# A hybrid decoder layer on one core: x handed over a second time with k on the partitions, norm factors as columns, row scale later

## The chip, the cores and the metric

The kernel runs on one core of one Trainium2 chip. It uses five engines: TensorE (PE) multiplies 128x128 weights with up to 512 columns and writes to PSUM, VectorE (DVE) and ScalarE (ACT) do element-wise work, GpSimd (POOL) makes masks and issues some transfers, and SyncE (SP) issues most transfers. In this kernel the operand that PE loads first ("LDWEIGHTS") is a block of activations, and the model's weights stream past it. The metric is the device time in microseconds (us) of one execution.

## The reference

One decoder layer, sequence 256, width 2048, float32. Cut to what matters here:

```python
h = rmsnorm(x, g_mix)                      # x * rsqrt(mean(x*x) + eps) * g_mix
proj = h @ w_in                            # 2048 x (3 * 2048 + 3 * 2048)
q, k, v = ...                              # 16 heads of 128
gates = sigmoid(proj[..., 3 * MIX_WIDTH:]) # three gates of 2048 channels
o_a = stick_breaking_attention(q[:, :4], k[:, :4], v[:, :4])
qn, kn = rmsnorm(q[:, 4:], q_gain), rmsnorm(k[:, 4:], k_gain)
o_b = moba_attention(...)                  # 6 heads, with a relative-position bias
o_c = dilated_attention(...)               # 6 heads, with a relative-position bias
merged = sum of gates[i] * (o_i @ w_branch[i])
x = x + merged @ w_out
gu = rmsnorm(x, g_ffn) @ w_gu
x = x + (silu(gu[..., :D_FF]) * gu[..., D_FF:]) @ w_down
```

## The kernel before, in words

All matrix products keep float32 accuracy by splitting each operand into a high part (a rounding cast to the type fp32r, on ACT) and a low part (the rest, subtracted on DVE), and adding three products: high x high, high x low, low x high (`product`, lines 159 to 162). A weight tile is two k-tiles of 128 rows by 512 columns (512 KB), loaded on SP into one of four `w_raw` buffers, split into five `w_hi` and five `w_lo` buffers (`split`, line 106), and used for two row tiles of 128 tokens. So a k-tile costs PE six matmuls.

`h` holds the activations with k on the partitions, as high and low parts: 16 k-tiles of 128 rows by 256 tokens. The norm is applied in two pieces. The channel factor g_mix multiplies x on the way into `h`; the token factor `rstd` (one number for each row) is applied later, to the results in PSUM, since a row scale commutes with the product. `rstd` comes from sums of squares of x as rows (`squares`, on ACT), a reduction and `rsqrt_mean` (a logarithm, an exponential and two refinement steps, DVE and ACT in turn).

The input projection goes in units: V of the heads 0 to 3, a gate chunk, Q and K of heads 0 to 3, and so on (`units`). V and gate units are plain (`project`); two units side by side use one level of a seven-product scheme on k-tiles 0 to 7 (`project_pair`, begun early by `begin_pair`), whose sums of activations are made by `sums_of_h` from the k-tiles times g_mix. Four PSUM banks (`ps`, `qs`, two of each) take turns; V unit 0 has `ps`, gate unit 0 `qs`, and the first Q/K pair `ps` again, so that pair cannot begin before V has been read out and scaled by `keep_v`.

x arrives as rows. Each of its eight pieces (128 tokens by 512 channels) is turned by four PE transposes through a PSUM tile `tr`, multiplied by g1 (g_mix as columns) on DVE, or on ACT for the last channels, and split. For the first four k-tiles the order of PE, DVE and ACT is written out by hand (lines 472 to 504: `high`, `low`, `first_columns`, `low_part`, `high_high`, `low_high`, `high_low`), weights coming one k-tile at a time. g_mix arrives as 16 rows of 128 and is turned by one PE transpose (line 446); the FFN factor and the gains of q and k arrive as 40 rows on POOL's queue and are turned later (line 591). `idle` puts filler matmuls of zeros on PE, five and then three.

Other work is cut into small steps (generators in `stages` and `slow_stages`) that are advanced once per k-tile or weight tile; a scheduler then orders each engine's instructions by its own estimate, apart from those marked `keep_in_program_order`. Transfers by `fetch` keep their place on SP.

Of the kernel before, what the change touches and what calls it, by code (L numbers as in the profile page):

```python
# [17 lines left out]
P = 128  # L18
D = 2048
S = 256  # L20
# [14 lines left out]
NDIST = 3 * P - 1  # L35

# [18 lines left out]
def hybrid_block(ctx: ExitStack, tc: tile.TileContext, x, g_mix, w_in, q_gain, k_gain, w_branch, w_out,  # L55
                 g_ffn, w_gu, w_down, rel_bias, onehot, extra, out):
# [12 lines left out]
    consts.tile([P, 72], F32, name="fill")  # L69
    gmix = consts.tile([KT, P], F32, name="gmix")  # L70
    nc.scalar.dma_start(gmix, g_mix[0].rearrange("(k p) -> k p", p=P))
# [43 lines left out]
    def weights(w, row0, k0, nk, col0, there=()):  # L115

        for i, c in enumerate(range(k0, nk, 2)):
            raw = there[i] if i < len(there) else raw_weights(w, row0, c, col0)[0]
# [21 lines left out]
    def project(acts, k0, w, row0, nk, col0, ps=None, done=0, there=(), last=1):  # L140
# [4 lines left out]
        for k, w_hi, w_lo in weights(w, row0, done, nk, col0, there):  # L145
# [234 lines left out]

    NPAR = KT + 2 * H_SOFT
    par = consts.tile([NPAR, P], F32, name="par")
# [22 lines left out]
    def to_h(acts, src, c, t, g, by_scalar=False):  # L405

        pt = transpose4(src)
        tmp = half_kb().rearrange("p (k q) -> p k q", k=4)
        if by_scalar:
            for i in range(4):  # L410
                nc.scalar.activation(tmp[:, i], pt[:, i], AF.Copy, scale=g[:, 4 * c + i:4 * c + i + 1])
        else:
            nc.vector.tensor_mul(tmp, pt, g[:, 4 * c:4 * c + 4, None].to_broadcast([P, 4, P]))
        acts.put(c, t, tmp)
        return tmp

    def squares(xc, dst, c, pin=False):
        for t in range(NT):
            sq = nc.scalar.activation(half_kb(), xc[t], AF.Square, accum_out=dst[:, t, c:c + 1])
            if pin:  # L420
                tc.keep_in_program_order(sq)
# [3 lines left out]
    g1 = consts.tile([P, KT], F32, name="g1")  # L425
    g2 = consts.tile([P, KT], F32, name="g2")
# [4 lines left out]
    xc = [half_kb() for _ in range(NT)]  # L431
    xs = [xc]
    raws = [wpool.tile([P, 2, NB], F32, name="w_raw", bufs=4) for _ in range(2)]

    def first_weights(k):
        fetch(raws[k // 2][:, k % 2, :], w_in[k * P:(k + 1) * P, V0:V0 + NB])
# [8 lines left out]
    pg = tr.tile([P, 4 * P], F32, name="tr")  # L445
    nc.tensor.transpose(pg[:, :KT], gmix, ident[:KT, :KT])
    nc.vector.tensor_copy(g1, pg[:, :KT])
    xs.append(load_x(1, fetch))
    there = []
    for k in (4, 6):  # L450
        raw, issue = raw_weights(w_in, 0, k, V0)
        tc.keep_in_program_order(issue)
        there.append(raw)
    xs += [load_x(c, fetch) for c in (2, 3)]


    columns = {c: [o_raw[:, 4 * i + 2 * t:4 * i + 2 * t + 2, :].rearrange("p h (a q) -> p (h a) q", a=2)
                   for t in range(NT)] for i, c in enumerate(WC)}

    def next_columns(c, t, pt):  # L460
        tmp = columns[c][t]
        nc.vector.tensor_mul(tmp, pt, g1[:, 4 * c:4 * c + 4, None].to_broadcast([P, 4, P]))
        h.put(c, t, tmp)

    held = []

    def first_columns(t, n, w, goes_on=None):

        if not goes_on:
            held.append(tr.tile([P, 4, P], F32, name="tr"))  # L470
            for i in range(w):
                nc.tensor.transpose(held[-1][:, i, :], xc[t][:, (n + i) * P:(n + i + 1) * P], ident)
            if goes_on is not None:
                return
        pt = held[-1]
        k = slice(n, n + w)
        c = columns[0][t][:, k]
        nc.vector.tensor_mul(c, pt[:, 0:w], g1[:, k, None].to_broadcast([P, w, P]))
        nc.scalar.copy(h.hi[:, k, t * P:(t + 1) * P], c)

    def low_part(t):
        q = slice(t * P, (t + 1) * P)
        nc.vector.tensor_sub(h.lo[:, 0:4, q], columns[0][t], h.hi[:, 0:4, q].bitcast(F32))

    ps0 = banks()
    his, los = ([wpool.tile([P, 2, NB], F32R, name=f"w_{n}") for _ in range(2)] for n in ("hi", "lo"))
    W_HI, W_LO = ([t[k // 2][:, k % 2] for k in range(4)] for t in (his, los))
    RAW = [raws[k // 2][:, k % 2] for k in range(4)]
    how = dict(skip_group_check=True, stop=False)

    def high(k):
        nc.scalar.copy(W_HI[k], RAW[k])

    def low(k):
        nc.vector.tensor_sub(W_LO[k], RAW[k], W_HI[k].bitcast(F32))

    def high_high(t, k):
        nc.tensor.matmul(ps0[t], h.plain(t, k)[0], W_HI[k], start=k == 0, **how)

    def high_low(t, k):  # L500
        nc.tensor.matmul(ps0[t], h.plain(t, k)[0], W_LO[k], start=False, **how)

    def low_high(t, k):
        nc.tensor.matmul(ps0[t], h.plain(t, k)[1], W_HI[k], start=False, **how)

    with tc.manual_schedule(engines={mybir.EngineType.PE, mybir.EngineType.DVE, mybir.EngineType.Activation}):
        high(0)
        first_columns(0, 0, 2)
        first_columns(0, 2, 2)
        idle(3)  # L510
        high_high(0, 0)
        first_columns(1, 0, 4, False)
        low(0)
        high(1)
        high_high(0, 1)
        low_part(0)
        high_low(0, 0)
        low_high(0, 0)
        first_columns(1, 0, 4, True)
        low(1)  # L520
        low_high(0, 1)
        high_low(0, 1)
        turned = [transpose4(xs[1][0])]
        high_high(1, 0)
        high_high(1, 1)
        high_low(1, 0)
        high(2)
        low_part(1)
        high_low(1, 1)
        low_high(1, 0)  # L530
        low_high(1, 1)
        low(2)
        high_high(0, 2)
        low_high(0, 2)
        turned.append(transpose4(xs[1][1]))
        high_high(1, 2)
        low_high(1, 2)
        high(3)
        low(3)
        next_columns(1, 0, turned[0])  # L540
        high_low(0, 2)
        high_low(1, 2)
        high_high(0, 3)
        low_high(0, 3)
# [552 lines left out]
```

## Time and profile before

| | |
|---|---|
| median of 3 runs | 1434.06 us (1432.44 to 1434.29) |
| the profiled execution | 1433.64 us, span 1431.9 us |
| PE busy | 1421.7 us, 99% of the span |
| VectorE, ScalarE busy | 1196.0 us (84%), 882.0 us (62%) |
| PE's clock as granted | 1.00 |
| data moved | 310.09 MB, 217 GB/s on average |
| first product of V unit 0 | 7.23 us after the span's start |
| first product of the first Q/K pair | 56.49 us |

A row of the timeline has the start, the length, the engine, the line of the kernel, the operation, the tile written and the tiles read, the shape, a count of like instructions in a row, and in brackets the idle time before it and what ended that. PE's matmuls overlap, so their lengths do not add up: what one costs is the distance from its start to the next one's start. "PEld" is the loading of the operand that stays in place, "SPq" or "ACTq" the issue of a transfer by that engine. A row of the windows has, for each engine, the busy time in that stretch, then the clock, the share of the transfer engines and GB/s.

### The profile page before, as it was taken

To read this page: it belongs to the slowest core of one execution; us is meant where nothing else is said; L and a number is where in the kernel's file an instruction comes from. 1 tells how busy PE (TensorE), PEld (TensorE's weight loads), DVE (VectorE), ACT (ScalarE), POOL (GpSimd) and SP (SyncE) were. 2 spreads that over 40 slices of the span, in tenths; PEclk is the share of its full clock that TensorE was granted. 3 is DMA by queue.
4 is the path that set the end of the run, shared out by engine and by line. 5 is a ranking of instruction groups with operands and counts; after the bars stand their busy time and mean duration, and the time that the engine had idled before them with its cause. 6 is when DMAs were issued, how large, how long until landed. Compare 5 with 4: busy or idle time off the path is not lost. (4 is left out here: it accounts for less than half of the span.)

```text
span 1431.9 us, 17773 instructions
## 1 busy us (share of the span) xinstructions
PE 1421.7 (99%) x6404; PEld 1172.1 (82%) x6404; DVE 1196.0 (84%) x1262; ACT 882.0 (62%) x1140; POOL 72.6 (5%) x133
## 2 busy tenths in 40 slices
PE   9999999999999999999999999999999999999998
PEld 7888888888788888888888888888888888788887
DVE  7888787857999886776689999999999998886775
ACT  7667876766766665444456666666666666554453
POOL 1000000000000002100100000000000010100000
PEclk9999999999999999999999999999999999999999
DMA  8763647465666758866786657666665666767552
GB/s 270 264 218 119 220 127 247 122 221 173 215 203 238 257 194 291 278 224 211 223 299 224 224 206 251 216 225 229 219 217 191 231 212 223 256 230 240 190 169 97
DMA packets 154472, 310.09 MB, mean 217 GB/s; under 512 B 10672, under 2 KB 12288, under 8 KB 154384
## 3 DMA queue, kind: packets, MB, share of 16 engines
q1 hardware_dynamic: 143200, 275.29, 57.1%
q0 software_dynamic: 10000, 32.62, 6.5%
q10 hardware_dynamic: 1184, 1.06, 0.2%
q8 instruction: 50, 0.82, 0.2%
q14 instruction: 38, 0.31, 0.1%
HBM read 292.65 MB, written 16.27 MB: 216 GB/s over the span
## 5 line engine op out<-in xcount | busy, mean ns | idle before, releaser
L106 DVE TENSOR_TENSOR w_lo<-w_raw,w_hi 128x1024 fp32r<-128x1024 f32 x334 | 406.0, 1221 | 91.1 <-ACT w_hi L106 87.5
L106 ACT CAST w_hi<-w_raw 128x1024 fp32r<-128x1024 f32 x334 | 349.0, 1052 | 166.1 <-PE qs L162 67.4
L106 ACT CAST w_hi<-g_raw 128x1024 fp32r<-128x1024 f32 x184 | 192.6, 1053 | 120.4 <-PE ps L162 39.4
L106 DVE TENSOR_TENSOR w_lo<-g_raw,w_hi 128x1024 fp32r<-128x1024 f32 x184 | 219.6, 1220 | 36.1 <-ACT w_hi L106 35.2
L106 ACT CAST w_hi<-u 128x1024 fp32r<-128x1024 f32 x138 | 144.9, 1053 | 136.1 <-DVE u L303 65.1
L106 DVE TENSOR_TENSOR w_lo<-u,w_hi 128x1024 fp32r<-128x1024 f32 x138 | 166.5, 1221 | 37.0 <-ACT w_hi L106 35.6
L161 PE MATMUL ps<-w_lo,h_hi 128*128 128x512 f32 x360 | 140.9, 392 | 0.0
L162 PE MATMUL ps<-w_hi,h_lo 128*128 128x512 f32 x360 | 140.5, 390 | 0.0
L160 PE MATMUL ps<-w_hi,h_hi 128*128 128x512 f32 x360 | 137.5, 393 | 0.0
L161 PE MATMUL qs<-w_lo,h_hi 128*128 128x512 f32 x332 | 130.0, 392 | 0.8 <-DVE w_lo L106 0.8
L162 PE MATMUL qs<-w_hi,h_lo 128*128 128x512 f32 x332 | 129.6, 390 | 0.0
L160 PE MATMUL qs<-w_hi,h_hi 128*128 128x512 f32 x332 | 126.7, 391 | 0.0
L303 DVE TENSOR_TENSOR u<-u,g_raw 128x1024 f32<-128x1024 f32 x80 | 94.4, 1218 | 0.0
L162 PEld LDWEIGHTS ps<-w_hi,h_lo 128*128 128x128 f32 x360 | 67.6, 188 | 14.0
L161 PEld LDWEIGHTS ps<-w_lo,h_hi 128*128 128x128 f32 x360 | 67.6, 188 | 13.7
L160 PEld LDWEIGHTS ps<-w_hi,h_hi 128*128 128x128 f32 x360 | 67.5, 188 | 13.7
L161 PEld LDWEIGHTS qs<-w_lo,h_hi 128*128 128x128 f32 x332 | 62.4, 188 | 13.9 <-DVE w_lo L106 1.2
L162 PEld LDWEIGHTS qs<-w_hi,h_lo 128*128 128x128 f32 x332 | 62.4, 188 | 13.4 <-issue 0.6
L160 PEld LDWEIGHTS qs<-w_hi,h_hi 128*128 128x128 f32 x332 | 62.3, 188 | 12.7
L314 DVE TENSOR_TENSOR u<-g_raw 128x1024 f32<-128x1024 f32 x40 | 48.8, 1219 | 21.0 <-DMA g_raw<-in_w_in 16.2
L160 PE MATMUL v<-w_hi,h_hi 128*128 128x512 f32 x120 | 47.5, 396 | 0.2 <-ACT w_hi L106 0.2
L161 PE MATMUL v<-w_lo,h_hi 128*128 128x512 f32 x120 | 47.1, 393 | 0.0
(397 smaller groups left out, 2935.2 us busy)
## 6 DMA issues: line engine op xcount, KB each, us to landing
w_raw<-in_w_in SPq DMA_DIRECT2D x118, 512.0 KB, 4.6
g_raw<-in_w_gu SPq DMA_DIRECT2D x88, 512.0 KB, 5.1
w_raw<-in_w_gu SPq DMA_DIRECT2D x88, 512.0 KB, 6.4
g_raw<-in_w_in SPq DMA_DIRECT2D x72, 512.0 KB, 5.8
w_raw<-in_w_down SPq DMA_DIRECT2D x64, 512.0 KB, 4.6
w_raw<-in_w_branch SPq DMA_DIRECT2D x32, 512.0 KB, 5.1
w_raw<-in_w_out SPq DMA_DIRECT2D x32, 512.0 KB, 4.7
g_raw<-in_w_down SPq DMA_DIRECT2D x24, 512.0 KB, 5.3
```

Of the source, the lines that this page charges most:

```text
L106: for op in nc.scalar.copy(hi, src), nc.vector.tensor_sub(lo, src, hi.bitcast(F32)):
L160: nc.tensor.matmul(ps, ah, wh, start=start, stop=False, **how)
L161: nc.tensor.matmul(ps, ah, wl, start=False, stop=False, **how)
L162: nc.tensor.matmul(ps, al, wh, start=False, stop=stop, **how)
L303: tc.keep_in_program_order(nc.vector.tensor_add(d, d, a))
L314: nc.vector.tensor_add(d, a, b)
```

## The change

The program is handed two more arrays instead of four small ones: `xT`, x once more with the channel within a k-tile on the partitions (128 x 16 x 256), and `gains`, the norm factors and gains as 56 columns on 128 partitions.

- The 32 transposes of x and their copies are gone from the start. `xT` is loaded into `x_raw` (the memory of `o_raw`, which the attention fills later). ACT makes the high part as x times g1 rounded (`x_high`), DVE the low part as x times g1 minus the high part in one instruction (`x_low`), 256 columns each.
- g1, g2 and the gains are slices of the one tile `par`, loaded on ACT's queue. Their transposes on PE, their copies on DVE and three loads on POOL's queue are gone.
- The first eight k-tiles instead of four come one by one, x and weights in turn on SP. The hand-written order is the same for each: x high, weight high, x low, weight low, then six products. There are seven filler matmuls ahead of it instead of eight in two groups.
- The remaining eight k-tiles of x come in two transfers of four and are split one per step of V unit 0 (`rest_of_x`).
- x as rows is still needed for the sums of squares. It is loaded within gate unit 0 (`first_norm`), between its weights on SP, followed by the squares and `rsqrt_mean`; the scaling of V 0 (`scaled` in `keep_v`) comes after that, as a step of gate unit 0.
- `sums_of_h` multiplies `x_raw` by g1 in place, and splits a chunk for both row tiles in one instruction where it took two.

In the order as built, the relative-position bias table's three loads stand first on POOL's queue, its matmul stands between products of k-tile 3 and the addition after it ahead of the low part of weight tile 6; before, the table came in gate unit 0. From the end of the first Q/K pair on, every engine has the same instructions in the same order in both kernels.

```diff
+    consts.tile([P, 344], F32, name="fill")
+    par = consts.tile([P, NPAR], F32, name="par")
+    nc.scalar.dma_start(par, gains)
+    g1, g2, q_gain, k_gain = (par[:, a:b] for a, b in zip(PAR_AT, PAR_AT[1:]))
...
-    tc.keep_in_program_order(nc.gpsimd.dma_start(par[0:KT, :], g_ffn[0].rearrange("(k p) -> k p", p=P)))
-    tc.keep_in_program_order(nc.gpsimd.dma_start(par[KT:KT + H_SOFT, :], q_gain[0]))
-    tc.keep_in_program_order(nc.gpsimd.dma_start(par[KT + H_SOFT:NPAR, :], k_gain[0]))
...
+    FIRST = 8
+    raws, his, los = ([wpool.tile([P, 2, NB], dt, name=f"w_{n}", bufs=bufs) for _ in range(FIRST // 2)]
+                      for n, dt, bufs in (("raw", F32, 4), ("hi", F32R, 5), ("lo", F32R, 5)))
+    x_raw = o_raw
+    def fetch_x(k, n):
+        fetch(x_raw[:, k:k + n, :], xT[:, k:k + n, :])
-    fetch(xc[0], x[0:P, 0:NB])
-    first_weights(0)
-    fetch(xc[1], x[P:S, 0:NB])
-    for k in range(1, 4):
-        first_weights(k)
-    idle(5)
+    for k in range(FIRST):
+        fetch_x(k, 1)
+        fetch(RAW[k], w_in[k * P:(k + 1) * P, V0:V0 + NB])
+    fetch_x(FIRST, 4)
+    idle(7)
+    def x_high(k):
+        nc.scalar.activation(h.hi[:, k, :], x_raw[:, k, :], AF.Copy, scale=g1[:, k:k + 1])
+    def x_low(k):
+        nc.vector.scalar_tensor_tensor(h.lo[:, k, :], x_raw[:, k, :], g1[:, k:k + 1], h.hi[:, k, :].bitcast(F32),
+                                       op0=ALU.mult, op1=ALU.subtract)
...
+        for k in range(FIRST):
+            x_high(k)
+            nc.scalar.copy(W_HI[k], RAW[k])
+            x_low(k)
+            nc.vector.tensor_sub(W_LO[k], RAW[k], W_HI[k].bitcast(F32))
+            for lo, w in ((0, W_HI), (1, W_HI), (0, W_LO)):
+                for t in range(NT):
+                    nc.tensor.matmul(ps0[t], h.plain(t, k)[lo], w[k], start=k + lo == 0 and w is W_HI, **how)
     def rest_of_x():
+        fetch_x(FIRST + 4, 4)
+        for k in range(FIRST, KT):
+            x_high(k)
+            x_low(k)
+            yield
+    def first_norm():
+        rows = []
+        for c in range(4):
+            rows.append(load_x(c, fetch))
+            yield
+            if c:
+                squares(rows[c - 1], ss1, c - 1)
+            yield
+        squares(rows[3], ss1, 3)
+        yield
         sst = small.tile([P, NT], F32, name="sst", bufs=1)
         nc.vector.tensor_reduce(sst, ss1, op=ALU.add, axis=AX.X)
         rsqrt_mean(rstd, sst, D, NT)
+        yield
     def sums_of_h():
+        for _ in range(2):
+            yield
         for c in WC:
-            sums(*columns[c], True)
-            yield
-            for t in range(NT):
-                split(*[x[:, :, t * P:(t + 1) * P] for x in hs.s[c]], columns[c][t])
-                yield
+            chunk = x_raw[:, 4 * c:4 * c + 4, :]
+            tc.keep_in_program_order(nc.vector.tensor_mul(chunk, chunk, g1[:, 4 * c:4 * c + 4, None].to_broadcast([P, 4, S])))
+            yield
+            sums(*(chunk[:, :, t * P:(t + 1) * P] for t in range(NT)), True)
+            yield
+            split(*hs.s[c], chunk)
+            yield
...
     def keep_v(g, ps):
+        if g:
+            finish_stages(slow_stages)
         heads["v", g] = v = pa.tile([P, NT, NB], F32, name="v", bufs=1)
+        def scaled():
+            for t in range(NT):
+                nc.scalar.activation(v[:, t, :], ps[t], AF.Copy, scale=rstd[:, t:t + 1])
+            yield
         if g:
+            finish_stages([scaled()])
             slow_stages.append(attention(g, *heads["qk", g], v))
+        else:
+            stages.extend((first_norm(), scaled()))
```

More of the change, by code (lines that the diff above doesn't have):

```diff
@@ L113, in raw_weights, with weights @@
         return raw, nc.sync.dma_start(raw, src)
-    def weights(w, row0, k0, nk, col0, there=()):
-        for i, c in enumerate(range(k0, nk, 2)):
-            raw = there[i] if i < len(there) else raw_weights(w, row0, c, col0)[0]
+    def weights(w, row0, k0, nk, col0):
+        for c in range(k0, nk, 2):
+            raw = raw_weights(w, row0, c, col0)[0]
             hi = wpool.tile([P, 2, NB], F32R, name="w_hi")
@@ L138, in finish_stages, with project @@
             advance(queue)
-    def project(acts, k0, w, row0, nk, col0, ps=None, done=0, there=(), last=1):
+    def project(acts, k0, w, row0, nk, col0, ps=None, done=0, last=1):
         ps = ps or banks()
         held = []
-        for k, w_hi, w_lo in weights(w, row0, done, nk, col0, there):
+        for k, w_hi, w_lo in weights(w, row0, done, nk, col0):
             if k:
@@ L403, in load_x, with squares @@
         return xc
[L405 to L417, printed above, removed]
+    def squares(xc, dst, c):
@@ L446, in hybrid_block @@
[L446 to L479, printed above, removed]
@@ L500, in high_low @@
[L500 to L504, printed above, removed]
-    with tc.manual_schedule(engines={mybir.EngineType.PE, mybir.EngineType.DVE, mybir.EngineType.Activation}):
[L507 to L544, printed above, removed]
-        high_high(1, 3)
-        low_high(1, 3)
-        next_columns(1, 1, turned[1])
-        high_low(0, 3)
-        high_low(1, 3)
@@ L839, in hybrid_block @@
             keep_v(what, ps)
-            if what == 0:
-                slow_stages.append(sums_of_h())
         elif kind == "qk":
```

65 lines of the change are left out of this document (17 added, 48 removed).

## The prediction

> **What bounds the kernel now.** I read the page's table of engines first, then the waits of TensorE, then the timeline of the first 60 us, which is where the diff acts.
>
> ```profile
> PE 1421.7 (99%) x6404; PEld 1172.1 (82%) x6404; DVE 1196.0 (84%) x1262; ACT 882.0 (62%) x1140; POOL 72.6 (5%) x133
> ...
> PE qs L161 <- DVE w_lo L106: 1.4, 3, 0.8
> PE ps L160 <- ACT v L773: 0.6, 1, 0.6
> ```
>
> PE is busy 99%, and from 110 us to the end (the two wait rows are the largest there) it waits under 4 us in all. So PE is the bound everywhere after the start: work taken from PE, or an earlier first product, moves the end by as much, unless a new wait gives it back. A faster VectorE or ScalarE alone is worth nothing.
>
> ```profile
> 1.52 2.50 PE L378 MATMUL tr<-sc 128*128 128x512 f32 x5 [1.52 <-DVE sc L396]
> ...
> 5.18 0.62 ACT L492 CAST w_hi<-w_raw 128x512 fp32r<-128x512 f32 x1 [2.64 <-DMA w_raw<-in_w_in]
> ...
> 5.78 1.65 PE L378 MATMUL tr<-sc 128*128 128x512 f32 x3
> ...
> 7.31 0.62 ACT L492 CAST w_hi<-w_raw 128x512 fp32r<-128x512 f32 x1 [0.71 <-DMA w_raw<-in_w_in]
> ...
> 15.49 0.48 PE L160 MATMUL ps<-w_hi,h_hi 128*128 128x512 f32 x1
> ...
> 54.68 0.39 PE L161 MATMUL qs<-w_lo,h_hi 128*128 128x512 f32 x1
> ...
> 56.49 0.39 PE L160 MATMUL ps<-w_hi,h_hi 128*128 128x512 f32 x1
> ```
>
> The row at 15.49 is the first product of k-tile 4 of the first V unit. Until then PE has done 24 products (4 k-tiles, 2 row tiles, 3 each); the rest was filler, waiting and transposes. The row at 56.49 is the first product of the first Q/K pair, after V unit 0 and gate unit 0 (192 products). From the end of that pair on, the built order of every engine is the same in both kernels, so the forecast is: when does that product start in the changed kernel?
>
> **What leaves PE, and what stays.**
>
> ```profile
> 16.27 0.40 PE L160 MATMUL ps<-w_hi,h_hi 128*128 128x512 f32 x1
> ...
> 18.11 0.39 PE L162 MATMUL ps<-w_hi,h_lo 128*128 128x512 f32 x1
> 18.34 1.03 PE L182 MATMUL tr<-ident,sc 128*128 128x128 f32 x8
> 19.13 0.48 PE L160 MATMUL ps<-w_hi,h_hi 128*128 128x512 f32 x1
> ...
> 23.58 0.60 PE L182 MATMUL tr<-ident,sc 128*128 128x128 f32 x4
> 23.93 0.48 PE L161 MATMUL ps<-w_lo,h_hi 128*128 128x512 f32 x1
> ...
> 25.27 0.25 PE L591 MATMUL tr<-ident,par 40*128 40x40 f32 x1
> ...
> 37.70 0.81 PE L605 MATMUL tr<-sc 32*12 32x383 f32 x2
> ```
>
> A product costs its spacing, not its duration: 16.27 to 18.11 is 8 steps, 0.23 us each; 54.68 to 56.49 again 8, 0.226 each. Eight transposes cost 19.13 - 18.34 = 0.79 us, four 23.93 - 23.58 = 0.35. After 15.49 the change so removes 1.14 us for twelve transposes and about 0.25 for the parameter one. The other twenty and that of the factors stood before 15.49. The bias-table matmul (0.81 us) stays; it moves from 37.70 to between two products of k-tile 3. So the changed kernel needs, from its first product to the first Q/K product, 96 x 0.23 + 96 x 0.226 + 0.8 = 44.6 us.
>
> **When the first product can start.** Its inputs: x k-tile 0 (128 KB, SP's first issue), weight tile 0 (SP's second, as before), and now the factors, one DMA of 128 rows of 224 bytes on ACT's queue, for ScalarE multiplies x by them.
>
> ```profile
> 0.81 0.38 SPq L103 DMA_DIRECT2D sc<-in_x  x1
> ...
> 2.18 1.38 SPq L103 DMA_DIRECT2D w_raw<-in_w_in  x3
> ...
> 5.76 0.83 ACT L479 CAST h_hi<-o_raw 128x256 fp32r<-128x256 f32 x2
> ...
> DMA to landing us min/median/max: 3.9/5.4/7.2
> ...
> DMA to landing us min/median/max: 3.3/3.3/3.3
> ...
> DMA to landing us min/median/max: 4.2/4.8/5.2
> ```
>
> The three landing rows are the first weights, the factors (ACT's queue) and the q, k and FFN gains (POOL's). Weight tile 0 landed by 5.18 and its cast took 0.62, so the first product can start at 5.8. The factors, issued at 0.81, land at 4.1 by their own row and at 6.0 by the slowest gains row; then come the x cast (0.42, half of the 0.83 row) and the weight cast: first product at 5.8 or at 7.0. I take 5.8, the row of the same queue. VectorE has to form gq ahead of its first low part; that hides behind the casts.
>
> The later k-tiles: two issues each at 0.46 us (1.38 / 3), the weights of tile k issued at 0.81 + 0.46 (2k + 1), landing 5.4 later, cast 0.62. Tile 1 is ready at 8.2, tile 3 at 10.1, tile 7 at 14.4 with VectorE's 0.68. PE wants them at 5.8 + 1.38k, so at 7.2, 9.9 and 15.5: late by 1.0 at tile 1, then early. ScalarE's (0.42 + 0.62) and VectorE's (0.40 + 0.60) work per tile is under PE's 1.38.
>
> **The cold start.** The filler matmuls at 5.78 still stand (1.65 - 0.79) / 2 = 0.43 us apart, nearly twice 0.23, and products come at full pace only from about 8.1; the page's clock row shows tenths of full speed and hides this. Products from 5.8 to 8.1 at 0.43 are 5.3 instead of 10: 4.7 x 0.23 = 1.1 us lost. That covers the lateness of tile 1, and ends at nothing if seven fillers in a row warm PE sooner. The Trainium skill, "TensorE: Matmul & The Clock Gate", Part 1, says that a busy window of some 3.4 us opens the clock and that the window runs free; by it the loss would lie between nothing and all of that, from run to run, and the spacing row agrees with its half rate.
>
> **VectorE's new order.** Eight tensor multiplies and eight low parts of 512 columns become sixteen low parts of 256 (one fused multiply-subtract each), and the sums' chunks are multiplied in place, pinned in order.
>
> ```profile
> 19.34 0.68 DVE L413 TENSOR_TENSOR sc<-tr,g 128x512 f32<-128x512 f32 x1
> 19.94 1.22 DVE L106 TENSOR_TENSOR w_lo<-w_raw,w_hi 128x1024 fp32r<-128x1024 f32 x1
> ...
> 29.37 0.42 DVE L203 TENSOR_TENSOR o_raw<-o_raw 128x256 f32<-128x256 f32 x1
> 29.71 0.69 DVE L106 TENSOR_TENSOR h_lo<-sc,h_hi 128x512 fp32r<-128x512 f32 x1
> ...
> 47.26 1.22 DVE L314 TENSOR_TENSOR u<-g_raw 128x1024 f32<-128x1024 f32 x1
> 48.39 2.49 DVE L106 TENSOR_TENSOR w_lo<-g_raw,w_hi 128x1024 fp32r<-128x1024 f32 x2
> ...
> L939 DVE SCALAR_TENSOR_TENSOR sc<-sc,rstd x22: 743/746/748, 779.2 to 1199.9; 128x512 f32<-128x512 f32 x22
> ```
>
> By spacing, 512 columns cost 0.60, 256 cost 0.34, 1024 cost 1.13; the fused form takes 0.06 more than 0.68 at 512, so 0.40 at 256. The built order puts, after the low part of weight tile 7 (14.4), eight x low parts, the weights of tiles 8-9, a chunk multiply, one sum and only then the weights of tiles 10-11: 8 x 0.40 + 3 x 1.13 + 0.34 = 6.9, ready at 21.3. PE wants it after 62 products and the table matmul: 5.8 + 1.1 + 0.8 + 62 x 0.23 = 22.0. It is hidden by 0.7; with the slowest landing (7.2) it comes 1.1 late. I charge 0.3 for this and tile 1 together.
>
> **What moves later, and the queues.** x is read a second time, as rows, for the norm: 2.1 MB more, pinned on SP between the weights of gate unit 0.
>
> ```profile
> 5.00:10.00 5.00, 4.47 (x17) 3.06 (x16) 3.57 (x7) 2.89 (x6) 0.00 (x0) 1.00 0.99 349
> ...
> 15.00:20.00 5.00, 5.00 (x30) 4.21 (x29) 4.65 (x8) 4.01 (x7) 0.00 (x0) 1.00 1.00 368
> ...
> 25.00:30.00 5.00, 5.00 (x23) 3.92 (x22) 4.03 (x9) 4.03 (x12) 0.37 (x1) 1.00 0.78 249
> 30.00:35.00 5.00, 5.00 (x24) 4.14 (x23) 3.70 (x9) 5.00 (x12) 1.19 (x3) 1.00 0.52 159
> ...
> sc<-in_x SPq DMA_DIRECT2D x8, 256.0 KB, 6.1
> ```
>
> The last two columns are DMA share and GB/s. The transfers are full until 20 us and then wait for buffers, so the added 2.1 MB / 368 GB/s = 5.7 us fall where there is room, and queue ahead of weights that are loaded up to nine k-pairs early. I cost them at nothing; uncovered, at most 5.7. POOL loses three parameter DMAs and issues the bias table's at once, so the bias rows come early too.
>
> The scaling of V now waits for the norm factor inside gate unit 0, and it holds the two PSUM banks that the Q/K pair needs.
>
> ```profile
> 33.91 0.15 DVE L562 TENSOR_REDUCE sst<-ss 128x2 f32<-128x8 f32 x1
> ...
> 46.59 0.15 DVE L176 TENSOR_TENSOR rstd<-rs_y,rs_t 128x2 f32<-128x2 f32 x1
> 46.77 1.26 ACT L773 ACTIVATE v<-ps,rstd 128x512 f32<-128x512 f32 x2
> ```
>
> Before, V was scaled by 48.0, 8.5 us ahead of 56.49. The order now places the last refinement behind the first two g_raw low parts and both u sums, as it almost did; the second g_raw cast needs the buffer of gate tiles 8-9, some 8 us before the pair. With about 1 for the cast, 1.13 for its low part, 2 x 1.13 for the sums and 1.3 for V, about 2 us of margin remain. Behind it on ScalarE stand the fourth g_raw cast and the gate's sigmoid, wanted later than V.
>
> **The sum.** 5.8 + 44.6 + 1.1 + 0.3 = 51.8 for the first Q/K product, against 56.49: 4.7 us less. The profiled execution took 1433.64 (span 1431.9 and 1.7 around it), so 1428.9; that execution lies 0.4 under the median of the three runs (1434.06). The likeliest case alone spans a gain of 3.3 (factors at 6.0, low part late) to 6.4 (no cold loss).
>
> **Rivals.** (a) *Transfers bound the first eight tiles.* For: tile 1 is late by 1.0 at the median landing and by 2.8 at the slowest, and if a 1 KB row of x costs as much as a 2 KB row, then 349 GB/s is 170 rows per us, and a tile's 256 rows take 1.5 us against PE's 1.38: 1.0 more over eight. First Q/K product 50.4 + 2.8 + 1.0 = 54.2, gain 2.3, 1431.3. Against: the queue ran at 349 to 368 GB/s with pieces no larger than 512 KB. The Trainium skill, "DMA: Bandwidth & Descriptors", Rules for kernel authors, speaks for it: it wants transfers of a MiB and warns of those below 64 KB; the trace's 256 KB pieces do not bear that out while several are under way. (b) *VectorE becomes the bound* up to the Q/K pair: the same work in 5 us less, with its wait for a cast before each low part; half the gain goes, 1431.3 or more. Against: two fewer PSUM-sourced multiplies per chunk, and 1.3 of 5 us idle at 30 to 35. (c) *The norm factor comes too late*: the other side. The last x rows stand on SP behind the weights of gate tiles 8-9. If these are fetched only at PE's pace, at 30.1 (V unit 0 done: 5.8 + 1.1 + 0.3 + 0.8 + 22.1) + 8 x 1.38 = 41.1, the rows land 6.1 later at 47.2, the chain (12.7 us from 33.91 to 46.59) and the 1.3 for V end at 61.2, and the pair starts 4.7 later than before: 1438.3. It costs the whole gain once V is scaled after 56.5. Against: loads run nine pairs ahead.
>
> **How the numbers follow.** Runs before differ by 1.9 us; about 0.2% (2.9 us) can be told from no change. Likeliest case 0.69, gain over 2.9 nearly throughout; (a) 0.15, half of it within 0.2%; (b) 0.08, within; (c) 0.08, slower. Faster 0.69 + 0.08 = 0.77, same 0.07 + 0.08 = 0.15, slower 0.08. The range runs from a gain of 6.6 with the spread of the runs (1426.6) to just past (a) and (b), 1431.8; (c) is left out.
>
> **What would show it.** Right: no transposes before the first product; first product near 5.8; products 0.23 apart from about 8 us; the first Q/K product near 51.8. Wrong: PE waiting for w_raw or w_hi in the first 12 us (a), for w_lo of tiles 8 to 11 or later (b), or ps waiting for ACT's v before the pair (c).

## The result and the profile after

The changed kernel took 1429.75 us (median of 11 runs, 1427.26 to 1431.51), the kernel before 1433.68 on the same chip (11 runs, 1430.8 to 1434.69): a ratio of 0.9975, 95% interval 0.9967 to 0.9983. By the ratio that is 3.6 us less, between 2.4 and 4.7; the two medians lie 3.93 us apart. The profiled execution after took 1427.99 us with a span of 1426.3; before it was 1433.64 and 1431.9. The two spans differ by 5.6 us, more than the medians: single executions of either kernel scatter by about 4 us, and the one profiled after lies 1.8 under its median. The part of the difference that lies at the start is read from the timeline below.

The table of engines of the changed kernel, then its waits of TensorE from 0 to 110 us:

```profile
PE 1416.0 (99%) x6369; PEld 1167.9 (82%) x6369; DVE 1195.1 (84%) x1262; ACT 883.1 (62%) x1139; POOL 71.1 (5%) x130
```

```profile
PE ps L164 <- DVE w_lo L109: 1.2, 1, 1.2
PE ps L444 <- ACT w_hi L439: 0.4, 1, 0.4
```

PE is still busy 99%. There are two waits after the fillers: 0.4 us for the weights of k-tile 1, and 1.2 us for the low part of the weights of k-tile 10 (`ps`, line 164, the first V unit), which the kernel before did not have. The timeline of the changed kernel shows both in place:

```profile
3.32 0.51 ACT L428 ACTIVATE h_hi<-o_raw,par 128x256 fp32r<-128x256 f32 x1 [0.78 <-DMA par<-in_gains]
4.06 0.62 ACT L439 CAST w_hi<-w_raw 128x512 fp32r<-128x512 f32 x1 [0.23 <-DMA w_raw<-in_w_in]
...
4.73 1.20 PE L444 MATMUL ps<-w_hi,h_hi 128*128 128x512 f32 x2
5.75 0.64 PE L444 MATMUL ps<-w_hi,h_lo 128*128 128x512 f32 x2
...
7.29 0.74 PE L444 MATMUL ps<-w_hi,h_hi 128*128 128x512 f32 x2 [0.43 <-ACT w_hi L439]
...
14.34 1.72 ACT L428 ACTIVATE h_hi<-o_raw,par 128x256 fp32r<-128x256 f32 x4 [0.67 <-DMA o_raw<-in_xT]
...
17.03 1.22 DVE L109 TENSOR_TENSOR w_lo<-w_raw,w_hi 128x1024 fp32r<-128x1024 f32 x1 [0.45 <-ACT w_hi L109]
...
18.40 0.41 PE L164 MATMUL ps<-w_lo,h_hi 128*128 128x512 f32 x1
...
18.57 1.22 DVE L474 TENSOR_TENSOR o_raw<-o_raw,par 128x1024 f32<-128x1024 f32 x1
...
20.71 0.61 PE L163 MATMUL ps<-w_hi,h_hi 128*128 128x512 f32 x2
20.89 0.42 DVE L206 TENSOR_TENSOR o_raw<-o_raw 128x256 f32<-128x256 f32 x1
21.23 2.35 DVE L109 TENSOR_TENSOR w_lo<-w_raw,w_hi 128x1024 fp32r<-128x1024 f32 x2
22.50 0.50 PE L164 MATMUL ps<-w_lo,h_hi 128*128 128x512 f32 x1 [1.17 <-DVE w_lo L109]
...
49.28 1.27 ACT L680 ACTIVATE v<-ps,rstd 128x512 f32<-128x512 f32 x2 [0.90 <-DVE rstd L179]
...
52.10 0.39 PE L163 MATMUL ps<-w_hi,h_hi 128*128 128x512 f32 x1
```

The factors are there at 3.32, weight tile 0 at 4.06, and the first product starts at 4.73. VectorE multiplies the sums' chunk (18.57) and forms a first sum (20.89) ahead of the low part of k-tiles 10 and 11 (21.23), so PE stands from 21.2 to 22.5. The first Q/K product comes at 52.10 instead of 56.49: 4.39 us earlier. Of that, 2.50 lie ahead of the first product (7.23 to 4.73) and 1.89 between it and the first Q/K product (49.26 us before, 47.37 after). A scaling on ScalarE of the results in `qs` (line 693, before line 781) that stands at 145.54 before comes at 141.12, 4.42 earlier; this second mark is used below.

The transfers, in windows of 10 us; the last two columns are DMA share and GB/s. First the kernel before, then the changed one:

```profile
20.00:30.00 10.00, 10.00 (x47) 7.99 (x46) 8.33 (x14) 9.03 (x22) 0.37 (x1) 1.00 0.79 240
30.00:40.00 10.00, 10.00 (x44) 7.51 (x43) 8.38 (x16) 7.75 (x16) 1.70 (x4) 1.00 0.69 215
```

```profile
20.00:30.00 10.00, 8.83 (x39) 6.98 (x38) 8.42 (x13) 6.14 (x10) 0.00 (x0) 1.00 1.02 318
30.00:40.00 10.00, 10.00 (x46) 8.29 (x45) 7.73 (x12) 8.66 (x18) 0.00 (x0) 1.00 1.00 371
```

The second reading of x fills the room that the kernel before had between 20 and 40 us.

### The profile page after: what moved, and what is told of

It is laid out like the page before. It is cut to its first block, busy times and chain, and to the rows that moved or that the text cites. A ratio compares the mean times of both kernels' runs of the same rounds, so it can differ in the third digit from the quotient of the medians.

```text
span 1426.3 us, 17715 instructions
## 1 busy us (share of the span) xinstructions
PE 1416.0 (99%) x6369; PEld 1167.9 (82%) x6369; DVE 1195.1 (84%) x1262; ACT 883.1 (62%) x1139; POOL 71.1 (5%) x130
## 4 chain that ended last, share of the span: by engine, by line
PE 83%; DVE 2%; issue 1%; ACT 1%; DMA 0%; DVEq 0%; SPq 0%; ACTq 0%
PE ps L164 10%; PE ps L163 10%; PE ps L165 10%; PE qs L164 9%; PE qs L165 9%; PE qs L163 9%; PE z L165 4%; PE z L164 4%; PE z L163 4%; PE v L163 3%; PE v L164 2%; PE v L165 2%; PE tr L164 1%; PE tr L165 1%; PE tr L163 1%; PE tr L185 1%
## 5 line engine op out<-in xcount | busy, mean ns | idle before, releaser
L164 PE MATMUL ps<-w_lo,h_hi 128*128 128x512 f32 x352 | 137.8, 391 | 1.2 <-DVE w_lo L109 1.2
L165 PE MATMUL ps<-w_hi,h_lo 128*128 128x512 f32 x352 | 137.2, 390 | 0.0
L163 PE MATMUL ps<-w_hi,h_hi 128*128 128x512 f32 x352 | 133.3, 392 | 0.0
L164 PEld LDWEIGHTS qs<-w_lo,h_hi 128*128 128x128 f32 x332 | 62.4, 188 | 13.9 <-DVE w_lo L109 1.2
L317 DVE TENSOR_TENSOR u<-g_raw 128x1024 f32<-128x1024 f32 x40 | 48.7, 1220 | 20.8 <-DMA g_raw<-in_w_in 16.3
L306 DVE TENSOR_TENSOR g_raw<-g_raw 128x1024 f32<-128x1024 f32 x40 | 47.1, 1219 | 0.0
```

Of the source, the lines that this page charges most:

```text
L163: nc.tensor.matmul(ps, ah, wh, start=start, stop=False, **how)
L164: nc.tensor.matmul(ps, ah, wl, start=False, stop=False, **how)
L165: nc.tensor.matmul(ps, al, wh, start=False, stop=stop, **how)
L306: tc.keep_in_program_order(nc.vector.tensor_add(d, d, a))
L317: nc.vector.tensor_add(d, a, b)
```

## The experiments

All are edits of the changed kernel, which computes the same in each. "First Q/K" and "141 mark" are the two places named above, from one profile each; ratios are to the kernel before on the same chip.

| kernel | ratio, 95% | first product | first Q/K | 141 mark |
|---|---|---|---|---|
| changed kernel | 0.9975, 0.9967 to 0.9983 | 4.73 | 52.10 | 141.12 |
| sums two steps later | 0.9974, 0.9963 to 0.9986 | 4.77 | 50.44 | 140.43 |
| sums one step later | 0.9973, 0.9962 to 0.9984 | 4.68 | 52.26 | 142.86 |
| no fillers | 0.9982, 0.9973 to 0.9991 | 4.86 | 51.75 | 140.66 |
| g_mix as rows | 0.9984, 0.9974 to 0.9993 | 6.41 | 54.50 | 143.51 |
| four k-tiles one by one | 1.0014, 1.0005 to 1.0023 | 5.24 | 59.18 | 148.10 |
| x rows loaded twice | 1.0000, 0.9991 to 1.0009 | 5.21 | 56.00 | 146.96 |
| norm early, bias late | 1.0007, 0.9998 to 1.0016 | 4.68 | 53.42 | 147.15 |
| norm early, bias first | 0.9966, 0.9952 to 0.9979 | 4.71 | 52.58 | 141.63 |
| bias late alone | 0.9972, 0.9963 to 0.9982 | 4.69 | 54.77 | 144.10 |
| norm early, sums one step later | 0.9961, 0.9947 to 0.9974 | 4.72 | 51.53 | 140.67 |

One more row of each timeline orders the table: the first low product of k-tile 10 (22.50 in the changed kernel). From there to the first Q/K product it takes 29.60 us in the changed kernel, and 29.46 to 29.64 in seven of the ten others. So what these eight differ in at the first Q/K product arose before k-tile 10, to within 0.2 us. With the bias table late it takes 30.3 to 30.6, because the table matmul (0.8 us) then stands on this stretch; with the rows loaded twice it takes 33.21.

The theory after the result: the gain is the earlier and denser start; VectorE's order at k-tile 10 takes back 1.2 to 1.3 us of it; the norm's new place and its 2.1 MB cost nothing. Rivals: the cold clock sets the start, not VectorE; the factors as columns matter little; the second reading of x or the later norm takes something back.

### Sums of activations two steps later

```diff
     def sums_of_h():
-        for _ in range(2):
+        for _ in range(4):
             yield
```

> The changed kernel with the multiplied chunks of the sums two steps later, so that VectorE makes the low part of weight tiles 10-11 ahead of the first chunk multiply. My theory (VectorE's order at k-tiles 8 to 11 costs PE its one longer wait after the first tiles, 1.2 us): that wait goes, and the first Q/K product starts at 50.7 to 51.2 us instead of 52.1; the time comes 1 us lower, 1428 to 1429. Rival (PE is held by the transfers there, the order only names the waiter): the wait stays at 0.8 or more, the start stays within 0.3 of 52.1. A second rival: the sums are now late for the Q/K pair and PE waits there as long as it gained.

Its timeline:

```profile
16.68 1.23 DVE L109 TENSOR_TENSOR w_lo<-w_raw,w_hi 128x1024 fp32r<-128x1024 f32 x1 [0.45 <-ACT w_hi L109]
...
19.40 3.49 DVE L109 TENSOR_TENSOR w_lo<-w_raw,w_hi 128x1024 fp32r<-128x1024 f32 x3
...
50.44 0.39 PE L163 MATMUL ps<-w_hi,h_hi 128*128 128x512 f32 x1
...
55.03 1.05 ACT L109 CAST b_shi<-o_raw 128x1024 fp32r<-128x1024 f32 x1
...
56.46 1.06 ACT L109 CAST w_hi<-w_raw 128x1024 fp32r<-128x1024 f32 x1
...
61.54 0.39 PE L163 MATMUL ps<-w_hi,b_shi 128*128 128x512 f32 x1
62.44 0.50 PE L164 MATMUL ps<-w_lo,b_shi 128*128 128x512 f32 x1 [0.51 <-DVE w_lo L109]
```

The wait at k-tile 10 is gone, and the first Q/K product comes 1.66 us earlier, a little more than the wait itself; 0.2 of it is that PE came to k-tile 10 a little earlier in this execution. From the low part of k-tiles 8 and 9 to that of 10 and 11 VectorE takes 2.72 us (16.68 to 19.40) instead of 4.20 (17.03 to 21.23): the multiply and the sum, 1.13 and 0.34 by their spacing, are gone from there. So VectorE's order set that wait. But inside the pair a new wait appears: PE comes to a low part at 61.8 that it gets at 62.4. VectorE starts it at the same time as in the changed kernel (61.16 against 60.98), though PE is 1.66 earlier: the second chunk is split only now, its cast on ScalarE at 55.03 and its low part on VectorE at 56.49, both ahead of the pair's weights, where the changed kernel has them before the pair. The weight cast behind it ends at 57.5 and the second chunk's low part at 57.6, so it is as much ScalarE's order as VectorE's. Whether the pair's weights would have been there sooner otherwise, the run doesn't tell. At the 141 mark 0.7 of the 1.66 us is left, which the timing can't separate from nothing.

### One step later

```diff
-        for _ in range(2):
+        for _ in range(3):
```

> The sums of activations begin one step later than in the changed kernel (three instead of two empty steps). VectorE then has the first chunk's multiply ahead of k-tile 10's low part, but no longer the first sum. If VectorE's order there sets the start: the wait for that low part falls from 1.2 us to 0.3 to 0.9, the first Q/K product comes at 51.0 to 51.8, and as the second chunk's low part keeps its place, no wait of 0.5 appears in the pair; time 0.5 to 1 us below the changed kernel, 1428.5 to 1429.5, which this many runs can hardly tell. Rival: PE loses as much at the next low part, and the first Q/K product stays at 52.1.

```profile
22.62 0.50 PE L164 MATMUL ps<-w_lo,h_hi 128*128 128x512 f32 x1 [0.82 <-DVE w_lo L109]
...
62.81 0.50 PE L163 MATMUL ps<-w_hi,b_shi 128*128 128x512 f32 x1 [0.76 <-ACT w_hi L109]
```

A miss. The wait shrank to 0.82 as expected, but PE also came later to it (tile 1 was ready 0.23 later in this execution), and the product behind it started at 22.62, not earlier than 22.50. VectorE shows why: it began the low part of k-tiles 8 and 9 at 17.49 instead of 17.03, after a later cast, and needed 3.86 us from there to that of 10 and 11 (21.35) instead of 4.20. So one step is worth one sum, 0.34 us, and the later cast took it back. The same 3.86 stands in the last experiment, and 4.19 in three kernels that leave the order alone. The pair has a wait of 0.76, for a weight cast.

### No fillers

```diff
-    idle(7)
+    idle(0)
```

> The changed kernel without its seven filler matmuls (nothing of the computation is left out). Theory of the cold start (the fillers open PE's clock before the products): the first products stand 0.43 us apart until about 8 us, and as tile 1 is late by itself until 7.3, the first Q/K product comes 0.5 to 1.5 us later than 52.1. Rival (the fillers have no part in it, the transfers pace the first tiles): within 0.3 of 52.1.

```profile
4.86 1.22 PE L444 MATMUL ps<-w_hi,h_hi 128*128 128x512 f32 x2 [4.86 <-ACT w_hi L439]
5.88 1.05 PE L444 MATMUL ps<-w_hi,h_lo 128*128 128x512 f32 x2
6.73 1.05 PE L444 MATMUL ps<-w_lo,h_hi 128*128 128x512 f32 x2
...
22.14 0.50 PE L164 MATMUL ps<-w_lo,h_hi 128*128 128x512 f32 x1 [0.53 <-DVE w_lo L109]
```

The half pace came as expected, its price did not. The products run at half pace for 3 us (0.85 to 1.02 for two, instead of 0.46), and still the first Q/K product, at 51.75, isn't later: tile 1 is no longer waited for, and the wait at k-tile 10 falls from 1.17 to 0.53. As long as VectorE is late at k-tile 10, what PE loses ahead of it costs nothing. That the mark is even 0.35 earlier isn't owed to the fillers: x of k-tiles 8 to 11 landed at 13.98 instead of 14.34 in this execution, and VectorE began the low part of k-tiles 8 and 9 as much earlier (16.67 instead of 17.03).

### g_mix as rows again

```diff
+    gmix = consts.tile([KT, P], F32, name="gmix")
+    nc.scalar.dma_start(gmix, g_mix[0].rearrange("(k p) -> k p", p=P))
...
     idle(7)
+    pg = tr.tile([P, 4 * P], F32, name="tr")
+    nc.tensor.transpose(pg[:, :KT], gmix, ident[:KT, :KT])
+    nc.vector.tensor_copy(g1, pg[:, :KT])
```

> The changed kernel with one part undone: g_mix comes again as 16 rows and is turned by one PE transpose and one copy; x still comes with k on the partitions. Theory (the first tile waits for the factors, but the second tile's late weights take up most of the delay): the first product starts near 6.3 us instead of 4.7, the first Q/K product 0.3 to 0.7 us later than 52.1. Rival (the factors set the start): the whole 1.6 us shows. Other rival (worth nothing): within 0.2.

```profile
4.81 0.28 PE L430 MATMUL tr<-ident,gmix 16*128 16x16 f32 x1
...
5.34 0.51 ACT L434 ACTIVATE h_hi<-o_raw,g 128x256 fp32r<-128x256 f32 x1 [2.33 <-DVE g L431]
...
6.41 1.22 PE L450 MATMUL ps<-w_hi,h_hi 128*128 128x512 f32 x2 [1.31 <-ACT w_hi L445]
...
13.37 0.90 PE L450 MATMUL ps<-w_hi,h_hi 128*128 128x512 f32 x2
14.11 0.63 PE L450 MATMUL ps<-w_hi,h_lo 128*128 128x512 f32 x2
...
54.50 0.39 PE L165 MATMUL ps<-w_hi,h_hi 128*128 128x512 f32 x1
```

The factors are usable at 5.34 instead of 3.32, so the first product comes 1.68 us later, and then PE runs at half pace for another 7 us. Together 2.40 us at the first Q/K product, although no wait at k-tile 10 is left. The built order differs a little, too: the table matmul stands among the first six products, where it costs 1.4 us instead of 0.8, and the first sum comes behind the low part of k-tiles 10 and 11. So by this mark, in one execution of each, handing over the factors as columns is worth about half of the start's gain: through the landing, and through the slow products, as far as VectorE's wait at k-tile 10 had not hidden them. The ratios (0.9984 and 0.9975) don't separate the two kernels. That the slow products come from PE's idle 1.3 us ahead of them is argued; no run shows it alone.

### Four k-tiles one by one instead of eight

```diff
-    FIRST = 8
+    FIRST = 4
...
-        fetch_x(FIRST + 4, 4)
+        for k in range(FIRST + 4, KT, 4):
+            fetch_x(k, 4)
         for k in range(FIRST, KT):
```

> Four k-tiles instead of eight come one by one; x of k-tiles 4 to 7 comes as one piece of 512 KB, weights from tile 4 on as pairs of 512 KB, all x ahead of the weights of tiles 6 and 7. If it matters that the pieces are small (a pair must be all there, and cast in one 1.03 us instruction, before its first product): first product unchanged at 4.7, then TensorE waits for the high and the low part of tiles 4 and 6 by 1 to 3 us each, and the first Q/K product comes at 53.5 to 56, the median at 1431 to 1434. The built order of VectorE also has both chunk multiplies ahead of the low part of tiles 6 and 7, which adds up to 2.3 us there. If VectorE's wait at k-tile 10 would have come anyway and absorbs this, it stays at 52.1 to 53 and 1429 to 1430.

```profile
13.19 0.73 PE L163 MATMUL ps<-w_hi,h_hi 128*128 128x512 f32 x2 [0.41 <-ACT w_hi L109]
14.45 0.50 PE L164 MATMUL ps<-w_lo,h_hi 128*128 128x512 f32 x1 [0.53 <-DVE w_lo L109]
...
18.55 1.22 DVE L475 TENSOR_TENSOR o_raw<-o_raw,par 128x1024 f32<-128x1024 f32 x1
...
20.09 1.22 DVE L109 TENSOR_TENSOR w_lo<-w_raw,w_hi 128x1024 fp32r<-128x1024 f32 x1
21.36 0.79 PE L164 MATMUL ps<-w_lo,h_hi 128*128 128x512 f32 x1 [3.29 <-DVE w_lo L109]
```

This is slower than the kernel before. The first product came 0.51 later in this execution, from inputs that the edit leaves alone. The pieces of 512 KB cost about 1.4 us at k-tile 4. The larger part is VectorE's order: between the low parts of tiles 4 and 6 (13.17 and 20.09) stand eight x low parts, both chunk multiplies and one sum; PE waits 3.29 us, and then runs at half pace until about 27. So the run shows that the part "eight one by one" is needed, but most of its worth here is the order of VectorE that comes with it, not the size of the pieces.

### x rows loaded twice

```diff
-            rows.append(load_x(c, fetch))
+            rows.append(load_x(c, fetch)); load_x(c, fetch)
```

> Each x row piece is loaded twice in its place, the second copy into a buffer that nobody reads: 2.1 MB more, on SP between the weights of gate unit 0. If the second reading of x costs nothing because weights are loaded far ahead, a third costs no wait of TensorE before the first Q/K product either: that product at 51.8 to 52.5 and the factor at most 2 us later. If the transfers have no room (they are at about 1.0 busy from 25 to 45 us), 2.1 MB at 368 GB/s push what follows by 5.7 us: the sum of squares is ready at 43 to 44 instead of 38.4, V is scaled at 54 to 56 and the first Q/K product comes 2 to 4 us later, at 54 to 56.

Its waits of PE from 0 to 110 us, then its timeline:

```profile
PE qs L164 <- DVE w_lo L109: 1.9, 4, 0.6
```

```profile
35.52 1.05 ACT L109 CAST w_hi<-w_raw 128x1024 fp32r<-128x1024 f32 x1 [1.44 <-DMA w_raw<-in_w_in]
37.89 0.50 PE L164 MATMUL qs<-w_lo,h_hi 128*128 128x512 f32 x1 [0.53 <-DVE w_lo L109]
```

Another 2.1 MB takes the whole gain: ratio 1.0000. The place is not the one that the rival named: the norm factor is no later (49.19 against 49.09). It is the weights of gate unit 0: casts wait for transfers, and PE waits four times for a low part, 2.8 us by the distances of its products. (The first product was also 0.48 later here, before any row is loaded.) The transfers are full from 20 to 50 us (DMA share 0.98 to 1.05 in each 5 us), where the changed kernel has 0.76 in the last 5. So the second reading of x, which adds no wait in the changed kernel, has used up the lead of the weights; a third has none.

### The place of the norm and of the bias table

First the norm (`first_norm`) into V unit 0 and V scaled at once; the bias table's loads then come after it:

```diff
-    stages.append(rest_of_x())
+    stages.extend((rest_of_x(), first_norm()))
...
-            stages.extend((first_norm(), scaled()))
+            finish_stages([scaled()])
```

> The changed kernel with the later row scale undone: x as rows is loaded within V unit 0, the norm follows there, and V is scaled at once. My theory (the added 2.1 MB fall behind weights that are loaded early, and the place of the norm costs PE nothing either way): first Q/K product within 0.5 us of 52.1, rstd some 5 us or more before 49.1. Rival (the rows collide with the weights in the first 20 us, where the transfers are full): PE waits for w_hi or w_lo in V unit 0 or gate unit 0, 1 us or more, up to 2.1 MB / 400 GB/s = 5 us.

The factor was ready at 47.33, only 1.8 us earlier, and the median no better than before. PE's timeline shows three waits inside the Q/K pair, and after them products 0.43 apart until 70:

```profile
62.74 0.50 PE L164 MATMUL qs<-w_lo,h_hi 128*128 128x512 f32 x1 [0.76 <-DVE w_lo L109]
...
65.03 0.50 PE L163 MATMUL ps<-w_hi,b_shi 128*128 128x512 f32 x1 [0.88 <-ACT w_hi L109]
66.29 0.50 PE L164 MATMUL ps<-w_lo,b_shi 128*128 128x512 f32 x1 [0.76 <-DVE w_lo L109]
...
67.32 0.63 PE L164 MATMUL ps<-w_lo,b_shi 128*128 128x512 f32 x1
67.75 0.63 PE L165 MATMUL ps<-w_hi,b_slo 128*128 128x512 f32 x1
```

This edit moved two things, so each was tried alone. The norm early, but behind the bias table:

```diff
-    stages.append(parameters())
+    stages.extend((parameters(), first_norm()))
...
-            stages.extend((first_norm(), scaled()))
+            finish_stages([scaled()])
```

> The norm (x as rows, squares, factor) is put into V unit 0 and V is scaled at once, as in the run before, but the bias table's loads stay ahead of it, where the changed kernel has them. If the 4 to 6 us that the early norm lost came from its own place (row loads and squares among the start's weights), the loss stays: waits near 17 to 23 us of 2 us or more in sum, first Q/K product at 53.4 or later, the first scaling of q and k near 145 to 147 us, median near 1433. If it came from the bias rows that then ran beside the weights of the first Q/K pair, only the waits at the start are left: first Q/K product at 52.5 to 53.4, no cold TensorE at 60 to 70 us, scaling of q and k at 141 to 142.5, median 1429 to 1431.

The bias table late, and the norm as in the changed kernel:

```diff
-    stages.append(parameters())
...
-            stages.extend((first_norm(), scaled()))
+            stages.extend((first_norm(), scaled(), parameters()))
```

> The changed kernel with nothing moved but the bias table, which comes after the norm and the scaling of V, so that its rows are loaded near the first Q/K pair. If the late bias rows cost the 4 to 6 us of the run with the early norm: first Q/K product within 0.5 us of the changed kernel's 52.1, then waits for weights between 58 and 70 us of 3 us or more, scaling of q and k at 144 to 147 instead of 141.1, median 1432.5 to 1434. If the place of the norm cost them: no more than 1 us is lost here, and the median stays at 1429 to 1431.

> The late bias table once more, one look. In its first profile x of k-tiles 8 to 11 took 5.6 us from issue to landing instead of 3.9, ahead of any bias row, and TensorE waited 2.0 us for k-tile 8 and ran at half pace after it. If the place of the bias table causes that, it is there again: first Q/K product at 54 to 55. If that was a slow transfer by chance, the product comes at 51.5 to 53.

The early norm alone lost 0.5 us at both marks, nearly all of it before k-tile 10 (22.96 against 22.50), and no measurable time. So the row scale "later" neither wins nor loses time by itself: with the factor at 47.82 and V scaled from 48.34, the pair still starts when PE is done with the gate unit. But the built order kept the factor's last step late, so V was scaled only 0.9 us earlier than in the changed kernel (2.1 in the last experiment); a much earlier factor wasn't tried. The late bias table alone had no wait in the pair either. Its loss lay elsewhere, at k-tile 8 (first of two profiles, an execution of 1434.52 us, 3.6 above the median of its runs):

```profile
18.86 0.73 PE L163 MATMUL ps<-w_hi,h_hi 128*128 128x512 f32 x2 [1.95 <-ACT w_hi L109]
20.12 0.79 PE L164 MATMUL ps<-w_lo,h_hi 128*128 128x512 f32 x1 [0.53 <-DVE w_lo L109]
20.71 0.63 PE L165 MATMUL ps<-w_hi,h_lo 128*128 128x512 f32 x1
```

In the second execution profiled, of 1429.5 us, the wait at k-tile 8 was 0.70, PE did not slow down, and the first Q/K product came at 53.73, between the two expectations. x of k-tiles 8 to 11 landed at 16.17 and 15.15, against 14.34. Of the 1.63 us that this execution is behind the changed kernel, 0.80 stand at k-tile 10 (23.30 against 22.50) and 0.83 are the table matmul: it no longer stands ahead of k-tile 8, where PE's later wait would have hidden it, but right ahead of the first Q/K product. Ten timed runs give the same ratio as the changed kernel.

So neither move alone costs the 4.6 us (1.0007 against 0.9975) that the two cost together. The waits in the pair come only where both are made. Their cause is open, and one rival is left: the bias rows. With the early norm they were issued at 49.1, beside the pair's weights, which landed 12.4 us after their issue (median of those issued from 48 to 62) against 8.0 in the changed kernel (10.7, and no wait, with the norm early and the bias first); ScalarE's cast at 60.38 had waited 3.43 us for one. The bias late alone put the rows elsewhere, at 63.2 and 61.8, and there the weights took 6.0 and 5.4. So that experiment didn't try the place where the rows could hurt.

### Norm early and sums one step later

```diff
-        for _ in range(2):
+        for _ in range(3):
...
             chunk = x_raw[:, 4 * c:4 * c + 4, :]
             tc.keep_in_program_order(nc.vector.tensor_mul(...))
-            yield
             sums(...)
```

and `first_norm` placed as in the run with the bias table first.

> The two changes that cost nothing by themselves, put together: the norm in V unit 0 with V scaled at once, behind the bias table, and sums of activations one step later, without an empty step between a chunk's multiply and its sums. The wait at k-tile 10 falls from 1.2 to below 0.9 us, V is scaled 1 us or more earlier relative to the first Q/K product than in the changed kernel, no wait of 0.5 us appears in the pair: first Q/K product at 51.3 to 52.2, scaling of q and k at 140 to 141, time 0 to 1 us below the changed kernel, which a few runs can't tell. Rival: as in the two runs before, what PE gains at one low part it loses at the next, and these marks stay at 52.1 to 52.6 and 141 to 142.

```profile
21.89 0.50 PE L164 MATMUL ps<-w_lo,h_hi 128*128 128x512 f32 x1 [0.84 <-DVE w_lo L109]
...
51.53 0.39 PE L163 MATMUL ps<-w_hi,h_hi 128*128 128x512 f32 x1
```

As expected: the wait at k-tile 10 is 0.84, V is scaled from 47.16 instead of 49.28, there is no wait in the pair, and both marks come about half a microsecond earlier. It is the best ratio measured, but its interval overlaps that of the changed kernel: it beats the kernel before, and is not shown to beat the changed one.

## Why the prediction was right, point by point

- *The first Q/K product at 51.8, gain 4.7.* It came at 52.10, gain 4.39; the median gained 3.6 (2.4 to 4.7), the predicted median 5.2. The mechanism was right: a start that is earlier and denser, and that PE carries to the end. That the sum came out to 0.3 us is luck, because two wrong terms nearly cancel. It had 1.4 us of the gain ahead of the first product and 3.3 behind it; the trace has 2.50 and 1.89.
- *First product at 5.8.* Mis-sized: 4.73. The landing of weight tile 0 was taken from the row before (5.18), where 256 KB of x stood ahead of it; now 128 KB do, and it landed by 4.06 (3.9 to 4.6 in the experiments that keep this order). That the bytes ahead are the reason is argued, not tried alone. The factors, bounded by 4.1 and 6.0, were there by 3.32, below both ends. The run with g_mix as rows shows how much hangs on it: 1.68 us at the first product, 2.40 at the pair.
- *44.6 us of products from there.* 52.10 - 4.73 = 47.37, so 2.8 us were lost on the way, where 1.1 + 0.3 were charged. Up to k-tile 8's low part (18.40) PE had done 50 products and the table matmul in 13.67 us; at 0.23 and 0.8 these take 12.3. So cold start and tile 1 cost 1.4 together. (The table matmul came among the products of k-tile 2, counted from 0, not of k-tile 3 as was said; the sum is the same.)
- *The cold start, 1.1.* About 0.6 here (the first two products to 5.75 instead of 5.19), with a wait of 0.43, a gap of 0.6, for tile 1. That tile was ready at 7.3 where PE wanted it at 6.1, late by 1.2 instead of 1.0, and the cold start covered only half of that. In ten executions with the same fillers ahead of the products, products came at full pace from somewhere between 5.2 and 7.4 us on, so the prediction was right to expect this term to change from run to run. The run without fillers shows that its price was not independent: it is absorbed at k-tile 10.
- *VectorE's low part of k-tiles 10 and 11, hidden by 0.7.* This is the step that failed. It was wanted at 21.2, not 22.0, as PE began earlier, and ready at 22.4, not 21.3: x of k-tiles 8 to 11 landed only at 14.34, and the low part of tiles 8 and 9 waited for ScalarE until 17.03. The order and the price of VectorE's work were right; its two waits were left out (0.17 for the first of these x high parts, 0.45 for that cast). 1.3 us were lost where the step had nothing (0.3 with tile 1, and 1.1 "with the slowest landing"). The run with the sums two steps later returned 1.66.
- *2.1 MB more at no cost, at most 5.7 uncovered.* Right for this kernel: no wait of PE between 23 and 110 us. But the cover was thinner than the text let expect: the next 2.1 MB cost 2.8 us in waits and 3.9 at the pair.
- *V scaled with about 2 us to spare.* It was done at 50.55, 1.55 ahead of the pair, so rival (c) did not come. Scaling it 0.9 to 2.1 us earlier bought nothing that the runs can show.
- *The likeliest case, a gain of 3.3 to 6.4.* The upper end doesn't follow from its terms: without a cold start and without waits it is 56.49 - (5.8 + 44.6) = 6.1.
- *Rival (a), transfers bound the first eight tiles.* Only tile 1 waited. From 10 to 20 us the core moved 402 GB/s in pieces of 128 to 512 KB, so the rule from the Trainium skill, "DMA: Bandwidth & Descriptors", Rules for kernel authors, that transfers should reach a MiB, did not decide here.
- *Rival (b), VectorE becomes the bound up to the pair.* Right at one place, for 1.3 us, not for half the gain.

## What to carry to other kernels

When a start is made denser, list for every engine what now stands ahead of the first thing that PE will need, at PE's new and earlier times: here one multiply and one sum for a much later use cost 1.3 us, and moving them was worth 1.66 at the pair, 0.7 further on, and in the timed runs nothing that can be told from noise. A transfer that adds no wait has still spent a margin; adding the same bytes once more shows how much is left, here none. And, as far as one landing shows it, take a landing time from a row with the same bytes ahead of it in its queue, or let the range reach below it.

## What the hardware showed unexpectedly

How long PE is idle before it falls to half pace is not one number. A gap of 1.3 us after 14 us of dense work (21.2 to 22.5) left it at full pace. Two gaps of 2.1 and 0.8 us close together (16.8 to 20.1, bias late) left it at products 0.43 apart for 3 us, three gaps of about 1 us within 4.5 us (61.8 to 66.3, norm early and bias late) for 3.5 us, one of 3.3 us (four k-tiles one by one) for 6 us. The Trainium skill, "TensorE: Matmul & The Clock Gate", Part 1, has the clock fall after an idle window of about 3.4 us; in two of these runs it fell with work inside any such stretch. The length fits: in the traces' record of the granted clock the three slow stretches, all at 0.50, last 3.41, 3.41 and 6.83 us (from 20.2, 67.1 and 20.8 us on). What share of work keeps PE at full pace, these four cases don't tell.

What the seven fillers do can't be read from one execution. The views show the granted clock as 1.00 from the start, but its record begins only about where the products reach full pace, and the stretch before it counts as 1.00; the spacing of the products tells what it was. By the record full pace came at 6.1 us in the changed kernel, and anywhere from 4.9 to 7.8 in the ten executions that have the fillers and then the products at most 0.4 us later. With no fillers at all it came at 8.2, close behind that range. With g_mix as rows, where the products came 1.3 us after PE's last work, it came at 14.3: far outside the range, but that is one execution.
